# A two-layer transformer block on one core: silu(c) and the squares of the first norm in PSUM, the opening's steps in a written order, the low parts taken one and two feature tiles later

## The chip, the cores and the metric

The kernel runs on one core of one Trainium2 chip. The metric is the device time of one execution in microseconds. Before the change the median of three runs is 1338.73 us (1336.64 to 1339.17).

## What is computed

Two layers act on x of 512 tokens by 1024 features. Each layer has a modulation by a vector c (six parts of 1024 columns), four kinds of attention side by side, an output projection and an MLP. What matters here is the start of layer 0:

```python
c_act = jax.nn.silu(c)
mod = c_act @ w_ada[l] + b_ada[l]
sh1, sc1, g1, sh2, sc2, g2 = [t[:, None, :] for t in jnp.split(mod, N_ADA, axis=-1)]
h = rmsnorm(x, norm_mix_g[l]) * (1.0 + sc1) + sh1
z = h @ w_in[l]
za, zb, zc, zd = split_last(z, [SWA_COLS, MLA_COLS, NSA_COLS, MOBA_COLS])
```

rmsnorm divides by the root of the mean square over the features of a token. Everything is fp32. Products on TensorE are made from two parts of each operand, a high part rounded to fp32r and a low part that holds the rest, and three products stand for one: high by high, low of h by high of w, high of h by low of w.

## The kernel before, in words

The activations lie with features on partitions: x is eight tiles of 128 features by 512 tokens. The change is in the opening of layer 0, the function start (L1085 to L1155), which is called with n = 5: it makes h of all eight feature tiles and the first five groups of 128 columns of z, each in a PSUM bank of its own.

- **silu(c) spread out.** Eight small matmuls put silu(c) on every partition (cb, 128x1024); they land in two PSUM banks named cbp (L173), and DVE copies these to SBUF (L177).
- **x and weights.** The DMA queue of SP brings vecs, ident, x in four transfers, two raw weight tiles of w_in, then in turn raw weights and 16 tiles of w_ada: for each feature tile k a part 1 (the scale) and a part 0 (the shift). The raw weights have four buffers, the w_ada pairs (ada0) four. SP issues in program order, and an issue that waits for a buffer holds those behind it.
- **The norm.** ACT squares the tiles of x (L246), the first into sqacc, the others into SBUF tiles sq; DVE adds them to sqacc (L247). PE sums over partitions (nsum, L1098), DVE scales (rsv, L253), POOL takes the power -1/2 (rs, L257), PE spreads the result (rsb in PSUM, L263).
- **One feature tile.** ada_cols (L188) multiplies a w_ada tile by cb and sums along the row on DVE: one column of mod. Two such steps per feature tile; gs = (mod + 1) * norm weight (L1115); ht = x * gs * rsb (L1121); ACT adds the shift and rounds: hhi (L1124). For the first five tiles ACT writes ht + shift (L1126) and POOL makes hlo (L1127), for the last three DVE makes hlo (L1129).
- **One weight tile.** Weights._split: ACT rounds it (whi, L89), POOL takes the difference (wlo, L91, 128x1024). Eight weight tiles are split in the opening, five of them for it and three for later groups.
- **The products.** 120 matmuls of 128x128 by 512 columns: 5 groups, 8 feature tiles, 3 products. For tiles 0 to 4 they go tile by tile (high by high L1146, low of h L1148; the products with wlo, L1151, wait until tile 2 and then come for tiles 0 to 2 together); the last three tiles go group by group through mm3 (L330 to L332).

The order on an engine is that of a scheduler of the framework; issue_after(x) puts what follows behind x where both are on the same engine, and adds no wait between engines. Behind the opening, ACT and DVE take the five banks apart and PE goes on with the next weight groups (pn, L502).

Of the kernel before, what the change touches and what calls it, by code (L numbers as in the profile page):

```python
# [109 lines left out]
def layer_stack(ctx: ExitStack, tc: tile.TileContext, a, out):  # L110
# [7 lines left out]
    psA = ctx.enter_context(tc.tile_pool(name="psA", bufs=3, space=PSUM))  # L118
    psS = ctx.enter_context(tc.tile_pool(name="psS", bufs=2, space=PSUM))
    psT = ctx.enter_context(tc.tile_pool(name="psT", bufs=2, space=PSUM))  # L120
    psO = ctx.enter_context(tc.tile_pool(name="psO", bufs=1, space=PSUM))

    def mmbank(name):
        return psA.tile([P, 512], F32, tag="mm", name=name)
# [43 lines left out]
    cb = cons.tile([P, D], F32, name="cb")  # L168
    for half in range(2):
        ps = psA.tile([P, 512], F32, tag="mm", name="cbp")  # L170
        for j in range(4):
            k = 4 * half + j
            nc.tensor.matmul(  # L173
                ps[:, j * P : (j + 1) * P], cact[:, k : k + 1].to_broadcast([P, P]), ident,
                start=True, stop=True,
            )
        nc.vector.tensor_copy(cb[:, 512 * half : 512 * half + 512], ps)  # L177

# [5 lines left out]

    def ada_cols(w, l, part, m):

        off = l * VL + OFF_BADA + 8 * part + m
        nc.vector.tensor_tensor_reduce(  # L188
            out=w, in0=w, in1=cb, scale=1.0, scalar=vecs[:, off : off + 1],
            op0=ALU.mult, op1=ALU.add, accum_out=mod[l][:, part, m : m + 1],  # L190
        )

    def ada_start(pool, m):

        raw = pool.tile([P, 2, 1024], F32, tag="ada0", name="ada0", bufs=4)
        for part in (1, 0):
            nc.sync.dma_start(raw[:, part, :], a["wadaP"][m, :, part, :])
            ada_cols(raw[:, part, :], 0, part, m)

# [69 lines left out]
    def sbank(name):  # L269
        return psS.tile([P, 512], F32, tag="sc", name=name)  # L270
# [814 lines left out]
    def start(pool, n):  # L1085

        X["x"] = pool.tile([P, KT, S], F32, name="x0")
        sums = Sums()
        for k in range(0, KT, 2):
            nc.sync.dma_start(X["x"][:, k : k + 2, :], a["xT"][:, k : k + 2, :])  # L1090
        for _ in range(PRELOAD):
            W._load()
        for k in range(KT):
            sums.add(k)
        rsb = psO.tile([P, 512], F32, tag="po", name="rsb0")
        ps = sbank("nsum")
        for j in range(NQ):
            nc.tensor.matmul(  # L1098
                ps[:, j : j + 1], sums.acc[:, j * P : (j + 1) * P], ones, start=True, stop=True
            )  # L1100
# [4 lines left out]
        pss += [psT.tile([P, 512], F32, tag="pt", name="pj") for _ in range(min(n, 5) - 3)]  # L1105
        pss += [sbank("pj") for _ in range(n - 5)]
        W.other_pool.update({i: (pool, 4) for i in range(4)})
        ws = []
        gs = smp.tile([P, KT], F32, tag="gs", name="gs")
        for k in range(KT):  # L1110
            ada_start(pool, k)
            if k < n:
                W.split_ahead, W.load_ahead = AHEAD[k], LAHEAD[k]
                ws.append(W.get())
            nc.vector.scalar_tensor_tensor(  # L1115
# [17 lines left out]
        while W.n_split < n + NSPLIT:  # L1133
            W._split()
        load_consts()
        for _ in range(NADA):
            i = ada_state["i"]
# [5 lines left out]
            ada_state["i"] += 2  # L1143
        for k in range(KG):
            for g in range(n):
                nc.tensor.matmul(pss[g], ws[g][0][:, k, :], hs[k][0], start=k == 0, stop=False)  # L1146
            for g in range(n):
                nc.tensor.matmul(pss[g], ws[g][0][:, k, :], hs[k][1], start=False, stop=False)  # L1148
            for j in [k] if k >= KD else range(KD) if k == KD - 1 else []:
                for g in range(n):  # L1150
                    nc.tensor.matmul(pss[g], ws[g][1][:, j, :], hs[j][0], start=False, stop=False)  # L1151
# [166 lines left out]
```

## Time and profile before

| | |
|---|---|
| median of three runs | 1338.73 us (1336.64 to 1339.17) |
| the profiled execution | 1340.61 us |
| its span | 1338.8 us |
| PE busy | 1257.1 us, 94% |
| DVE busy | 765.2 us, 57% |
| ACT busy | 590.9 us, 44% |
| POOL busy | 512.1 us, 38% |

The span is the stretch from the first to the last instruction in the records of the profiled execution; 1.8 us of its time lie around it. PE is TensorE, DVE VectorE, ACT ScalarE, POOL GpSimd, and SP runs the DMA queue. The shares are means over the whole; the change touches the first 65 us or so. In the windows, the number behind a busy time is that of the instructions, PEclk is the granted clock of TensorE as a share of full speed.

### The profile page before, as it was taken

What the parts mean: (1) busy time and instruction counts of PE and PEld (TensorE: products, weight loads), DVE (VectorE), ACT (ScalarE), POOL (GpSimd) and SP (SyncE); (2) the same over time, 40 slices, a digit from 0 to 9 for tenths busy, and PEclk for the clock granted to TensorE, in tenths of its full rate; (3) what the DMA queues carried; (4) which work ended last, traced back from release to release, by engine and by line L of the source; (5) the groups of instructions that cost most, each with busy time, mean ns of one, the idle gap of its engine ahead of it and who ended that gap; (6) DMA issues with size and microseconds to landing.
All of it is one profiled execution on the core that took longest, in us unless ns stands there. A gap on an engine that the chain in (4) does not pass through costs nothing. (4 is left out here: it accounts for less than half of the span.)

```text
span 1338.8 us, 17560 instructions
## 1 busy us (share of the span) xinstructions
PE 1257.1 (94%) x6500; PEld 1049.3 (78%) x6500; DVE 765.2 (57%) x1609; ACT 590.9 (44%) x1145; POOL 512.1 (38%) x276
## 2 busy tenths in 40 slices
PE   3888999888999999999989899999999999999997
PEld 3676788768988888888889677878888888888886
DVE  6888878978445555454364887677753312213124
ACT  4346768683443132231234657687443313223220
POOL 4432232224344544545433432230534444444441
PEclk9989999999999999999989999999989999999999
DMA  8623233435246766766322221120423333333311
GB/s 334 209 98 127 64 111 111 140 126 206 69 131 185 244 212 209 239 190 204 130 93 90 94 95 64 51 74 11 166 80 94 94 95 95 96 97 98 102 49 64
DMA packets 49766, 168.69 MB, mean 126 GB/s; under 512 B 5648, under 2 KB 8336, under 8 KB 49680
## 3 DMA queue, kind: packets, MB, share of 16 engines
q1 hardware_dynamic: 49680, 167.57, 38.3%
q8 instruction: 51, 0.84, 0.2%
q14 instruction: 35, 0.29, 0.1%
HBM read 163.35 MB, written 4.19 MB: 125 GB/s over the span
## 5 line engine op out<-in xcount | busy, mean ns | idle before, releaser
L91 POOL TENSOR_TENSOR wlo<-raw,whi 128x1024 fp32r<-128x1024 f32 (+3 forms) x186 | 454.9, 2450 | 583.0 <-ACT whi L89 550.9
L89 ACT ACTIVATE whi<-raw 128x1024 fp32r<-128x1024 f32 (+3 forms) x186 | 193.7, 1045 | 437.7 <-PE px L331 237.5
L331 PE MATMUL pj<-hlo,whi 128*128 128x512 f32 (+1 forms) x783 | 297.3, 380 | 8.5 <-DVE hlo L295 8.4
L330 PE MATMUL pj<-hhi,whi 128*128 128x512 f32 (+1 forms) x783 | 296.0, 380 | 2.6 <-ACT hhi L1124 1.2
L332 PE MATMUL pj<-hhi,wlo 128*128 128x512 f32 (+1 forms) x783 | 294.7, 376 | 0.0
L330 PE MATMUL px<-a,whi 128*128 128x512 f32 (+1 forms) x560 | 208.4, 372 | 0.0
L332 PE MATMUL px<-a,wlo 128*128 128x512 f32 (+1 forms) x560 | 208.1, 372 | 0.0
L331 PE MATMUL px<-a,whi 128*128 128x512 f32 (+1 forms) x560 | 207.4, 370 | 0.0
L331 PEld LDWEIGHTS pj<-hlo,whi 128*128 128x128 f32 x783 | 150.8, 193 | 35.5 <-DVE hlo L295 11.4
L330 PEld LDWEIGHTS pj<-hhi,whi 128*128 128x128 f32 x783 | 150.4, 193 | 28.0 <-ACT hhi L1124 2.2
L332 PEld LDWEIGHTS pj<-hhi,wlo 128*128 128x128 f32 x783 | 150.7, 192 | 25.8
L368 DVE SCALAR_TENSOR_TENSOR x<-px,mod,x 128x512 f32<-128x512 f32 (+1 forms) x92 | 62.1, 678 | 171.1 <-PE px L332 162.1
L1071 DVE SCALAR_TENSOR_TENSOR t<-pj,r 128x512 f32<-128x512 f32 x64 | 44.3, 692 | 157.8 <-ACT r L1070 157.8
L188 DVE CUSTOM_DVE_ANT_0 adaw<-adaw,cb,vecs 128x1024 f32<-128x1024 f32 x78 | 105.2, 1349 | 43.8 <-DMA adaw<-in_wadaD 43.7
L332 PEld LDWEIGHTS px<-a,wlo 128*128 128x128 f32 x560 | 105.1, 188 | 19.2
L331 PEld LDWEIGHTS px<-a,whi 128*128 128x128 f32 x560 | 105.1, 188 | 18.8
L330 PEld LDWEIGHTS px<-a,whi 128*128 128x128 f32 x560 | 105.2, 188 | 17.9
L399 DVE TENSOR_TENSOR a<-t,a 128x512 fp32r<-128x512 f32 x64 | 71.8, 1122 | 44.7 <-ACT a L398 44.7
L540 ACT ACTIVATE e<-e,nm 128x256 f32<-128x256 f32 (+3 forms) x160 | 85.9, 539 | 14.6 <-DVE nm L535 14.4
L518 POOL TENSOR_SCALAR e<-e,rc 128x128 f32<-128x128 f32 x40 | 24.3, 608 | 143.2 <-DVE rc L545 67.1
L399 DVE TENSOR_TENSOR pl<-pt,ph 128x512 fp32r<-128x512 f32 (+1 forms) x112 | 65.3, 597 | 4.4 <-ACT ph L398 3.3
L574 PE MATMUL pt<-ident,e 128*128 128x128 f32 x376 | 61.7, 278 | 3.6 <-DVE pl L399 1.5
(236 smaller groups left out, 1932.7 us busy)
## 6 DMA issues: line engine op xcount, KB each, us to landing
adaw<-in_wadaD SPq DMA_DIRECT2D x78, 512.0 KB, 4.4
raw<-in_wup SPq DMA_DIRECT2D x64, 512.0 KB, 3.5
raw<-in_wdown SPq DMA_DIRECT2D x64, 512.0 KB, 3.5
raw<-in_winT SPq DMA_DIRECT2D x28, 512.0 KB, 3.6
ada<-in_wadaP SPq DMA_DIRECT2D x16, 512.0 KB, 7.2
raw<-in_wout SPq DMA_DIRECT2D x16, 512.0 KB, 3.5
x<-in_xT SPq DMA_DIRECT2D x8, 512.0 KB, 5.1
cw<-in_cw SPq DMA_DIRECT2D x8, 512.0 KB, 4.9
```

The source lines that it names most:

```text
L89: self.nc.scalar.activation(vh[0:rows], raw[0:rows], AF.Copy)
L91: eng.tensor_tensor(vl[0:rows], raw[0:rows], vh[0:rows].bitcast(F32), op=ALU.subtract)
L188: nc.vector.tensor_tensor_reduce(out=w, in0=w, in1=cb, scale=1.0, scalar=vecs[:, off : off + 1], op0=ALU.mult, op1=ALU.add, accum_out=mod[ ...
L330: nc.tensor.matmul(ps, wh[:, k, :], hh[:, c], start=first, stop=False)
L331: nc.tensor.matmul(ps, wh[:, k, :], hl[:, c], start=False, stop=False)
L332: nc.tensor.matmul(ps, wl[:, k, :], hh[:, c], start=False, stop=last)
L368: last["dve"] = nc.vector.scalar_tensor_tensor(X["x"][:, m, c], ps, mod[l][:, part, m : m + 1], X["x"][:, m, c], op0=ALU.mult, op1=ALU.add)
L399: last["dve"] = nc.vector.tensor_tensor(lo, src, hi.bitcast(F32), op=ALU.subtract)
L518: nc.gpsimd.tensor_scalar_mul(e, e, r)
L540: nc.scalar.activation(e, e, AF.Exp, bias=nm[:, n : n + 1], scale=-1.0, accum_out=den[:, n : n + 1])
L574: nc.tensor.transpose(pt[:, c : c + P], p[n][:, col : col + P], ident)
L1071: nc.vector.scalar_tensor_tensor(t, ps, 0.0, r, op0=ALU.max, op1=ALU.mult)
```

## The change: what it does

- cb stays in PSUM for the opening (cbP, two banks of a pool of its own, psC); ada_cols takes it as in0 and the w_ada tile in SBUF as in1. One ACT copy of 128x1024 (cb, behind the weight splits) fills the SBUF cb for the later w_ada tiles; then psC is closed and the pool psS takes its banks.
- The squares of tiles 1 to 7 go to PSUM (the three banks of psA), and DVE adds them from there; nsum takes a bank of psT.
- The weight splits of the opening are issued behind POOL's power, and ht of a tile behind both of its ada steps.
- PE takes the low part of h one feature tile after the high part, and the product with wlo two tiles after; the last tile's products and what is left go group by group, six in each.

```diff
-    psS = ctx.enter_context(tc.tile_pool(name="psS", bufs=2, space=PSUM))
...
     cb = cons.tile([P, D], F32, name="cb")
-    for half in range(2):
-        ps = psA.tile([P, 512], F32, tag="mm", name="cbp")
-        for j in range(4):
...
-        nc.vector.tensor_copy(cb[:, 512 * half : 512 * half + 512], ps)
...
-    def ada_cols(w, l, part, m):
+    def ada_cols(w, l, part, m, cv=cb):
...
-        nc.vector.tensor_tensor_reduce(
-            out=w, in0=w, in1=cb, scale=1.0, scalar=vecs[:, off : off + 1],
+        last["ada"] = nc.vector.tensor_tensor_reduce(
+            out=w, in0=cv, in1=w, scale=1.0, scalar=vecs[:, off : off + 1],
...
-        nc.gpsimd.tensor_tensor(r[:, 0:n], v[:, 0:n], mhalf[:, 0:n], op=ALU.pow)
+        last["pow"] = nc.gpsimd.tensor_tensor(r[:, 0:n], v[:, 0:n], mhalf[:, 0:n], op=ALU.pow)
...
+        psC = cps.enter_context(tc.tile_pool(name="psC", bufs=1, space=PSUM))
+        cbP = psC.tile([P, D], F32, name="cbP")
         for k in range(KT):
-            sums.add(k)
+            nc.tensor.matmul(
+                cbP[:, k * P : (k + 1) * P], cact[:, k : k + 1].to_broadcast([P, P]), ident,
+                start=True, stop=True,
+            )
+        acc = wkp.tile([P, S], F32, tag="sqacc", name="sqacc", bufs=1)
+        nc.scalar.activation(acc, X["x"][:, 0, :], AF.Square)
+        for k in range(1, KT):
+            sq = mmbank("sq")
+            nc.scalar.activation(sq, X["x"][:, k, :], AF.Square)
+            nc.vector.tensor_tensor(acc, acc, sq, op=ALU.add)
...
-            ada_start(pool, k)
+            ada_start(pool, k, cbP)
             if k < n:
                 W.split_ahead, W.load_ahead = AHEAD[k], LAHEAD[k]
-                ws.append(W.get())
+                with tc.issue_after(last["pow"].ins):
+                    ws.append(W.get())
...
-            last["dve"] = nc.vector.scalar_tensor_tensor(
-                t, X["x"][:, k, :], gs[:, k : k + 1], rsb, op0=ALU.mult, op1=ALU.mult
-            )
+            with tc.issue_after(last["ada"].ins):
+                last["dve"] = nc.vector.scalar_tensor_tensor(
+                    t, X["x"][:, k, :], gs[:, k : k + 1], rsb, op0=ALU.mult, op1=ALU.mult
+                )
...
+        nc.scalar.activation(cb, cbP, AF.Copy)
+        cps.close()
+        psS = ctx.enter_context(tc.tile_pool(name="psS", bufs=2, space=PSUM))
...
+        for k in range(KT - 1):
+            for w, j, h in ((0, k, 0), (0, k - 1, 1), (1, k - 2, 0)):
+                if j >= 0:
+                    for g in range(n):
+                        part(g, w, j, h)
+        k = KT - 1
         for g in range(n):
-            for k in range(KG, KT):
-                mm3(pss[g], ws[g], hs[k], k, False, k == KT - 1)
+            for w, j, h in (
+                (0, k - 1, 1), (1, k - 2, 0), (1, k - 1, 0), (0, k, 0), (0, k, 1), (1, k, 0)
+            ):
+                part(g, w, j, h)
```

**How it moves instructions.** Line numbers below are each kernel's own; an ISA row is ada_cols' step, a second short one the read of its sum.

POOL at the start of the opening; the first block is before, the second the change. wlo0 to wlo2 are the low parts of the first weight tiles, rs is the power, hlo the low part of feature tile 0.

```order
L91 TENSOR_TENSOR wlo0_208<-raw0_138,whi0_207 128x1024
L257 TENSOR_TENSOR rs_172<-rsv_170,mhalf_96 128x4
L91 TENSOR_TENSOR wlo1_212<-raw1_140,whi1_211 128x1024
L91 TENSOR_TENSOR wlo2_231<-raw2_205,whi2_230 128x1024
L1127 TENSOR_TENSOR hlo_179<-ht_216,hhi_178 128x512
```

```order
L246 TENSOR_TENSOR rs_169<-rsv_167,mhalf_93 128x4
L89 TENSOR_TENSOR wlo0_205<-raw0_122,whi0_204 128x1024
L89 TENSOR_TENSOR wlo1_209<-raw1_124,whi1_208 128x1024
L89 TENSOR_TENSOR wlo2_228<-raw2_202,whi2_227 128x1024
L1130 TENSOR_TENSOR hlo_176<-ht_213,hhi_175 128x512
```

The power now stands ahead of wlo0, the rest is as it was.

PE at the start of the products, before and then the change. hhi_178 and hlo_179 are the parts of feature tile 0 before, hhi_180 the high part of tile 1; in the change these are hhi_175, hlo_176 and hhi_177. whi0 to whi4 are the weight groups, pj their banks.

```order
L1146 MATMUL pj_194<-hhi_178,whi0_207 128x512
L1146 MATMUL pj_195<-hhi_178,whi1_211 128x512
L1146 MATMUL pj_196<-hhi_178,whi2_230 128x512
L1148 MATMUL pj_194<-hlo_179,whi0_207 128x512
L1148 MATMUL pj_195<-hlo_179,whi1_211 128x512
L1148 MATMUL pj_196<-hlo_179,whi2_230 128x512
L1146 MATMUL pj_197<-hhi_178,whi3_234 128x512
L1148 MATMUL pj_197<-hlo_179,whi3_234 128x512
L1146 MATMUL pj_194<-hhi_180,whi0_207 128x512
```

```order
L1151 MATMUL pj_191<-hhi_175,whi0_204 128x512
L1151 MATMUL pj_192<-hhi_175,whi1_208 128x512
L1151 MATMUL pj_193<-hhi_175,whi2_227 128x512
L1151 MATMUL pj_194<-hhi_175,whi3_231 128x512
L1151 MATMUL pj_191<-hhi_177,whi0_204 128x512
L1151 MATMUL pj_192<-hhi_177,whi1_208 128x512
L1151 MATMUL pj_193<-hhi_177,whi2_227 128x512
L1151 MATMUL pj_194<-hhi_177,whi3_231 128x512
L1151 MATMUL pj_191<-hlo_176,whi0_204 128x512
```

Before, the fourth product took the low part of tile 0; now eight products of high parts, of tiles 0 and 1, stand ahead of the first low part.

DVE behind the opening, before and then the change, between two casts and adds of the next stage (ckvg and ckl belong to the key part of one attention, mkh and mkl to its query part, VA to the values).

```order
L717 TENSOR_TENSOR ckvg_475<-ckvg_475,rkb_561 128x512
L487 TENSOR_TENSOR VA_493<-pn_571,VA_493 128x4x64
L399 TENSOR_TENSOR ckl_567<-ckvg_475,ckh_566 128x512
L668 TENSOR_TENSOR cB_681<-pj_198,vecs_85 64x8x31 x4
L487 TENSOR_TENSOR VA_493<-pn_599,VA_493 128x4x64
L668 TENSOR_TENSOR cB_683<-pj_198,vecs_85 64x8x31 x4
L754 CAST mkh_722<-cqh1_472 32x512
L755 CAST mkl_723<-cql1_473 32x512
L487 TENSOR_TENSOR VA_493<-pn_627,VA_493 128x4x64
```

```order
L706 TENSOR_TENSOR ckvg_477<-ckvg_477,rkb_563 128x512
L743 CAST mkh_724<-cqh1_474 32x512
L744 CAST mkl_725<-cql1_475 32x512
L388 TENSOR_TENSOR ckl_569<-ckvg_477,ckh_568 128x512
L476 TENSOR_TENSOR VA_495<-pn_573,VA_495 128x4x64
L657 TENSOR_TENSOR cB_683<-pj_195,vecs_82 64x8x31 x4
L657 TENSOR_TENSOR cB_685<-pj_195,vecs_82 64x8x31 x3
L476 TENSOR_TENSOR VA_495<-pn_601,VA_495 128x4x64
```

The two casts mkh and mkl now stand ahead of ckl and of the adds cB, where they stood behind them.

## Rows read from the trace of the kernel before

**Rows 1.** Windows: us; busy us (instructions) PE, PEld, DVE, ACT, POOL; PEclk, DMA share, GB/s.

```profile
0.00:25.67 25.67, 7.70 (x33) 7.06 (x33) 14.46 (x22) 10.01 (x15) 9.34 (x12) 1.00 0.93 353
25.67:39.90 14.23, 9.76 (x25) 6.09 (x25) 14.06 (x19) 5.38 (x7) 10.78 (x5) 0.88 0.58 186
39.90:64.80 24.90, 23.08 (x98) 17.89 (x98) 20.41 (x30) 10.58 (x17) 10.48 (x6) 1.00 0.73 257
```

**Rows 2.** Timeline of PE: the first products, and the last of the opening.

```profile
25.67 1.65 PE L1146 MATMUL pj<-hhi,whi 128*128 128x512 f32 x3 [4.38 <-ACT hhi L1124]
...
64.39 0.39 PE L332 MATMUL pj<-hhi,wlo 128*128 128x512 f32 x1
```

**Rows 3.** Timeline of DVE: start us, us, operation, [idle before].

```profile
9.88 5.03 DVE L247 TENSOR_TENSOR sqacc<-sqacc,sq 128x512 f32<-128x512 f32 x4
...
21.32 0.75 DVE L1121 SCALAR_TENSOR_TENSOR ht<-x,gs,rsb 128x512 f32<-128x512 f32 x1 [2.84 <-PE rsb L263]
21.99 2.86 DVE L188 CUSTOM_DVE_ANT_0 ada<-ada,cb,vecs 128x1024 f32<-128x1024 f32 x1
...
59.53 0.75 DVE L1129 SCALAR_TENSOR_TENSOR hlo<-ht,mod,hhi 128x512 fp32r<-128x512 f32 x1 [0.79 <-ACT hhi L1124]
```

**Rows 4.** Timeline of POOL in the first 25 us.

```profile
12.00 2.36 POOL L91 TENSOR_TENSOR wlo<-raw,whi 128x1024 fp32r<-128x1024 f32 x1 [11.00 <-ACT whi L89]
17.23 1.92 POOL L257 TENSOR_TENSOR rs<-rsv,mhalf 128x4 f32<-128x4 f32 x1 [2.87 <-DVE rsv L253]
19.12 4.65 POOL L91 TENSOR_TENSOR wlo<-raw,whi 128x1024 fp32r<-128x1024 f32 x2
```

**Rows 5.** One line's instructions: ns smallest/median/largest, first and last start us.

```profile
L188 DVE CUSTOM_DVE_ANT_0 ada<-ada,cb,vecs x16: 1274/1280/3409, 17.0 to 54.1; 128x1024 f32<-128x1024 f32 x16
L1115 DVE SCALAR_TENSOR_TENSOR gs<-mod,vecs x8: 155/708/2170, 18.3 to 56.0; 128x1 f32<-128x1 f32 x8
L1121 DVE SCALAR_TENSOR_TENSOR ht<-x,gs,rsb x8: 744/748/748, 21.3 to 58.0; 128x512 f32<-128x512 f32 x8
L535 DVE CUSTOM_DVE_ANT_0 e<-sc,biasN x64: 266/480/691, 149.6 to 868.0; 128x128 f32<-128x128 f32 x16, 128x256 f32<-128x256 f32 x16, 128x384 f32<-128x384 f32 x16, 128x512 f32<-128x512 f32 x16
```

**Rows 6.** DVE to 60 us, grouped by line: busy us, mean ns of one, idle before.

```profile
L188 DVE CUSTOM_DVE_ANT_0 ada<-ada,cb,vecs 128x1024 f32<-128x1024 f32 x16 | 25.1, 1590 | 0.0
L1115 DVE SCALAR_TENSOR_TENSOR gs<-mod,vecs 128x1 f32<-128x1 f32 x8 | 7.2, 902 | 0.1
```

**Rows 7.** Timeline of ACT: squares, a weight split, the first hhi.

```profile
9.59 1.15 ACT L246 ACTIVATE sq<-x 128x512 f32<-128x512 f32 x2 [0.37 <-DMA x<-in_xT]
...
16.37 1.06 ACT L89 ACTIVATE whi<-raw 128x1024 fp32r<-128x1024 f32 x1 [3.17 <-DMA raw<-in_winT]
...
24.89 0.72 ACT L1124 ACTIVATE hhi<-ht,mod 128x512 fp32r<-128x512 f32 x1 [7.46 <-DVE mod L188]
```

**Rows 8.** Windows, columns as in rows 1: 5 us of the opening.

```profile
15.00:20.00 5.00, 2.63 (x11) 2.58 (x12) 1.52 (x4) 1.06 (x1) 2.77 (x2) 1.00 1.02 417
```

**Rows 9.** Waits of the SP queue to 40.3 us: us, times, longest.

```profile
SPq L197 <- DVE mod L188: 19.0, 4, 7.2
```

**Rows 10.** Timeline of PE: five high by high products at two places.

```profile
37.49 2.50 PE L1146 MATMUL pj<-hhi,whi 128*128 128x512 f32 x5
...
45.25 1.32 PE L1146 MATMUL pj<-hhi,whi 128*128 128x512 f32 x5
```

**Rows 11.** Windows, columns as in rows 1: TensorE idle, and at work again.

```profile
31.70:35.65 3.95, 0.00 (x0) 0.00 (x1) 3.88 (x5) 0.00 (x0) 3.90 (x2) 1.00 0.35 135
36.49:39.90 3.41, 3.38 (x8) 1.75 (x6) 3.38 (x9) 1.44 (x2) 1.63 (x1) 0.50 0.57 154
```

**Rows 12.** Timelines of DVE and PE behind the opening.

```profile
82.65 2.58 DVE L755 CAST mkl<-cql 32x512 fp32r<-32x512 f32 x1
85.95 0.38 PE L734 MATMUL mv<-whi,ckh 128*128 128x256 f32 x1 [2.60 <-ACT gates L691]
...
88.30 0.58 PE L734 MATMUL mv<-whi,ckh 128*128 128x256 f32 x1 [1.74 <-DVE VM L487]
```

More of the change, by code (lines that the diff above doesn't have):

```diff
@@ L25 @@
 PRELOAD = 2
-KG = 5
 NSPLIT = 3
@@ L29 @@
 NJ0 = 1
-KD = 3
 NSTART = 5
@@ L118, in layer_stack @@
     psA = ctx.enter_context(tc.tile_pool(name="psA", bufs=3, space=PSUM))
-    psS = ctx.enter_context(tc.tile_pool(name="psS", bufs=2, space=PSUM))
     psT = ctx.enter_context(tc.tile_pool(name="psT", bufs=2, space=PSUM))
     psO = ctx.enter_context(tc.tile_pool(name="psO", bufs=1, space=PSUM))
+    psS = None
     def mmbank(name):
@@ L168, in layer_stack, with ada_start @@
     cb = cons.tile([P, D], F32, name="cb")
-    for half in range(2):
-        ps = psA.tile([P, 512], F32, tag="mm", name="cbp")
-        for j in range(4):
[L172 to L175, printed above, removed]
-            )
-        nc.vector.tensor_copy(cb[:, 512 * half : 512 * half + 512], ps)
     mod = [cons.tile([P, 6, KT], F32, name=f"mod{l}") for l in range(DEPTH)]
     W = Weights(nc, rawp, hlp, 3, 3)
-    def ada_cols(w, l, part, m):
+    def ada_cols(w, l, part, m, cv=cb):
         off = l * VL + OFF_BADA + 8 * part + m
-        nc.vector.tensor_tensor_reduce(
-            out=w, in0=w, in1=cb, scale=1.0, scalar=vecs[:, off : off + 1],
+        last["ada"] = nc.vector.tensor_tensor_reduce(
+            out=w, in0=cv, in1=w, scale=1.0, scalar=vecs[:, off : off + 1],
             op0=ALU.mult, op1=ALU.add, accum_out=mod[l][:, part, m : m + 1],
         )
-    def ada_start(pool, m):
+    def ada_start(pool, m, cv):
         raw = pool.tile([P, 2, 1024], F32, tag="ada0", name="ada0", bufs=4)
@@ L197, in ada_start @@
             nc.sync.dma_start(raw[:, part, :], a["wadaP"][m, :, part, :])
-            ada_cols(raw[:, part, :], 0, part, m)
+            ada_cols(raw[:, part, :], 0, part, m, cv)
     ada_todo = [(0, part, m) for part in (2, 4, 3, 5) for m in range(KT)]
@@ L1085, in start @@
     def start(pool, n):
+        nonlocal psS
         X["x"] = pool.tile([P, KT, S], F32, name="x0")
-        sums = Sums()
         for k in range(0, KT, 2):
@@ L1092, in start @@
             W._load()
+        cps = ctx.enter_context(ExitStack())
+        psC = cps.enter_context(tc.tile_pool(name="psC", bufs=1, space=PSUM))
+        cbP = psC.tile([P, D], F32, name="cbP")
         for k in range(KT):
-            sums.add(k)
+            nc.tensor.matmul(
[8 more added lines that the diff above has]
+            nc.vector.tensor_tensor(acc, acc, sq, op=ALU.add)
         rsb = psO.tile([P, 512], F32, tag="po", name="rsb0")
-        ps = sbank("nsum")
+        ps = psT.tile([P, 512], F32, tag="pt", name="nsum")
         for j in range(NQ):
             nc.tensor.matmul(
-                ps[:, j : j + 1], sums.acc[:, j * P : (j + 1) * P], ones, start=True, stop=True
+                ps[:, j : j + 1], acc[:, j * P : (j + 1) * P], ones, start=True, stop=True
             )
@@ L1105, in start @@
         pss += [psT.tile([P, 512], F32, tag="pt", name="pj") for _ in range(min(n, 5) - 3)]
-        pss += [sbank("pj") for _ in range(n - 5)]
         W.other_pool.update({i: (pool, 4) for i in range(4)})
@@ L1120, in start @@
             hi, lo = hs[k]
-            last["dve"] = nc.vector.scalar_tensor_tensor(
-                t, X["x"][:, k, :], gs[:, k : k + 1], rsb, op0=ALU.mult, op1=ALU.mult
-            )
+            with tc.issue_after(last["ada"].ins):
+                last["dve"] = nc.vector.scalar_tensor_tensor(
+                    t, X["x"][:, k, :], gs[:, k : k + 1], rsb, op0=ALU.mult, op1=ALU.mult
+                )
             nc.scalar.activation(hi, t, AF.Identity, bias=mod[0][:, 0, k : k + 1])
@@ L1143, in start, with part @@
             ada_state["i"] += 2
[L1144 to L1151, printed above, removed]
+        def part(g, w, k, h):
+            nc.tensor.matmul(
+                pss[g], ws[g][w][:, k, :], hs[k][h], start=(k + w + h == 0),
+                stop=(k == KT - 1 and w == 1),
+            )
+        for k in range(KT - 1):
[4 more added lines that the diff above has]
+        k = KT - 1
         for g in range(n):
-            for k in range(KG, KT):
-                mm3(pss[g], ws[g], hs[k], k, False, k == KT - 1)
+            for w, j, h in (
+                (0, k - 1, 1), (1, k - 2, 0), (1, k - 1, 0), (0, k, 0), (0, k, 1), (1, k, 0)
+            ):
+                part(g, w, j, h)
         return hs, pss
```

## The prediction

> **What bounds the kernel now.** I read the page first: TensorE is busy 94% of the span, so only a stretch in which it stands can give much. The slices show such a stretch at the start, so I read the windows of the opening, then PE's timeline, then DVE's, POOL's and ACT's. To 25.67 us PE does 7.70 us of work, from there to 39.90 it does 9.76 of 14.23, and DVE is busy 14.06 of the same 14.23 [rows 1]: DVE sets the pace. The first product starts at 25.67, after a wait of 4.38 for ACT's hhi; the last starts at 64.39 and takes 0.39, so the opening ends at 64.78 [rows 2], and PE goes straight on. What ends the opening sooner is gained at once, so far as later stages follow.
>
> Why is DVE so busy? Its adds of the squares: four take 5.03 us [rows 3], and in these POOL runs wlo0 from 12.00 to 14.36 [rows 4]. The 16 steps with cb have a median of 1280 ns and a largest of 3409; the eight gs, on one column each, run from 155 to 2170 [rows 5]. But the eight ht, which read rsb from PSUM, all take 744 to 748, and the reductions of L535, which read scores from PSUM, stay below 691 in 64 cases, all four sizes [rows 5]. One case: the step with cb that starts at 21.99 ends at 24.85, 1.1 after POOL's two splits, which run from 19.12 to 23.77 [rows 3, 4], as if most of its own 1.28 had to wait for them. My reading: a DVE instruction with all its tensors in SBUF waits for POOL's split to finish; one with an input in PSUM does not.
>
> **The change part by part.** The sum is made against the profiled execution, 1340.61 us, which is 1.9 above the median of the runs.
>
> 1. The squares in PSUM, and wlo0 behind the power. The last two squares run from 9.59 to 10.74 on ACT [rows 7]. One add unstretched is about 0.69 (an estimate from ht's 0.75, a two-tensor step of the same size [rows 5]), and it follows its square: the adds end near 11.5 instead of 14.91 (9.88 + 5.03 [rows 3]): -3.4. Were a PSUM input no help, wlo0 is still out of the way, as POOL's order shows, so this holds either way. The chain behind (nsum, rsv, power, rsb) took 21.32 - 14.91 = 6.41 and stays: ht of tile 0 starts at 17.9. The two cb copies drop out ahead of all this, beside the wait for x: nothing.
>
> 2. The first hhi. ht ended at 22.07, but hhi started at 24.89 [rows 7], for the shift's step stood behind ht and was stretched to 2.86 [rows 3]. In the change both steps of tile 0 come before ht, in the 2.84 that DVE waits for rsb. So hhi starts at about 18.7 and the first product at about 19.5 instead of 25.67 [rows 2].
>
> 3. DVE from ht of tile 0 to the last hlo: 21.32 to 60.28 (59.53 + 0.75 [rows 3]), 39.0 us. From this: the 16 steps fall from a mean of 1590 to the median, 16 x 0.31 = -5.0 [rows 5, 6]; one of them moves into the wait for rsb, -1.3; the gs still read SBUF alone, 8 x (0.902 - 0.155) = 6.0 of stretch [rows 5, 6]. Bounds: all of it stays, or all goes; since POOL does the same splits in less time I take half, -3.0. Added: the last hlo, from SBUF, now lies beside splits of the later weights, +1.5 (between 0 and the 2.36 of one split [rows 4]); the copy of cb stands on ACT ahead of the last hhi, priced by a weight split of the same 128x1024, 1.06 [rows 7], of which I take +0.7, as ACT is mostly idle. And SP: the fifth raw weight takes raw0's buffer, which wlo0 frees. wlo0 now ends behind the power, near 18.2 instead of 14.36, and everything behind that issue on SP, the w_ada pairs from tile 2 on among it, is held. The queue stays full meanwhile (DMA share 1.02 at 15 to 20 us [rows 8]), so this is bounded by 0 and 3.6 and taken as +1.0. The later pairs come sooner: SP waited 19.0 us for buffers that DVE frees [rows 9]. Sum: 39.0 - 5.0 - 1.3 - 3.0 + 1.5 + 0.7 + 1.0 = 32.9, so the last hlo ends at 50.8.
>
> 4. PE's tail. Behind the last hlo 26 products remain (two of the first group, six of four more), at a pitch of 0.232 ((1.32 - 0.39) / 4 [rows 2, 10]): 6.0, and 0.15 for the last one's length. Before, the tail was 64.78 - 60.28 = 4.5. The opening ends at 57.0 instead of 64.8: **-7.7**. The new order alone adds no product: 120 before and now. It moves low parts and wlo behind, so that PE no longer stands for POOL in front of high parts that are ready; as DVE is the pace, I count nothing beyond the dates above.
>
> 5. Behind the opening. The cast mkl of 32x512 took 2.58, over three times ht's 0.75 for 128x512 [rows 5, 12], which I read as the same stretch; PE waits 2.60 and 1.74 in the next microseconds [rows 12]. In the change both casts stand ahead of ckl. I take -1.0, between -4.3 (both waits go) and +2.0 (the two w_ada steps that follow the opening on DVE, about 1.3 each, fall in a worse place). The later w_ada steps read cb from SBUF as before: 0.
>
> Total -8.7: 1331.9 for a profiled execution, **1330.0** for the median.
>
> [...] In the rows, a reduction from PSUM at 512 columns takes at most 0.69 [rows 5], half of the 1.28 for 1024 columns from SBUF, so I put no surcharge into the sum. [...]
>
> **The rivals.**
>
> A. The change does not do what it says: a step that reads cb from PSUM and w from SBUF is stretched all the same, since one of its two inputs still comes from SBUF. For it: the 3409 ns step shows how much there is to lose, and no row before shows this very mix at 1024 columns. Against it: ht has the same mix (x from SBUF, rsb from PSUM) and stays at 744 to 748. Then DVE keeps its 39.0 us, with the same splits in it; the 3.4 of the adds and the 1.3 are eaten by later data (3.6) and the longer tail (1.5): about 1339, within 0.2%, up to 2.3 more where the stretch grows. Chance 0.07.
>
> B. The other side: TensorE at its low clock. It is fed sooner, but in small bursts with DVE's steps between. [...] Chance 0.05. [...]
>
> C. The gain is given back: PE comes to the attention stage 7.7 us sooner, and the waits at 82 to 92 us grow, as gates and the values' sums come from ACT and DVE, which have all the rest of their work to do. For it: PE waits there already [rows 12]. Against it: that work starts from the banks of the opening, so it moves forward too. With 5.5 to 7.5 given back: 1336 to 1338. Chance 0.12.
>
> **How the numbers follow.** My forecast has 0.76. Its unknowns all at their good ends (gs without stretch, both waits gone) give 1323.7; all at their bad ends (gs as before, data 3.6 late, +2.0 behind) 1338.6. They will not fall together, so I take 1324.5 to 1337.0; this takes in half of C and leaves out A, B and the other half, 0.18. About 0.2%, 2.7 us, is what a measurement can tell from no change: faster, under 1336.0, has the forecast and a quarter of C, 0.79; within 0.2% the rest of C and most of A, 0.14; slower B and the bad part of A, 0.07.
>
> **What would show it.** In the changed profile: adds at 0.7 each with the last ending near 11.5; 16 steps with cbP all near 1.28; ht of tile 0 at 17.9; a first product at 19.5; the last of the opening at about 57; PEclk 1.00 from 40 us on. I am wrong if the steps with cbP are stretched beside POOL (A), if PEclk shows 0.5 through the opening (B), if the opening ends near 57 and the waits for gates or VM have grown by as much (C), or if the w_ada tiles come so late that DVE waits for DMA.

## The result, and the profile of the changed kernel

The changed kernel takes a median of 1329.82 us (1328.21 to 1331.56, four runs); the kernel before took 1337.68 beside it (four runs). The ratio is 0.9943, with a 95% interval of 0.9924 to 0.9962: faster by 0.6%. The profiled execution of the change took 1331.56 us, 9.05 less than that of before; its span is 1329.8.

The windows of the opening, changed kernel, columns as in [rows 1]:

```profile
10.00:31.00 21.00, 12.05 (x34) 9.14 (x35) 18.23 (x27) 10.34 (x13) 16.26 (x9) 0.51 1.00 377
31.00:56.96 25.96, 24.52 (x106) 19.37 (x105) 20.67 (x33) 11.60 (x18) 8.82 (x6) 1.00 0.79 290
```

PE's timeline: the first products, the last wait of the opening, its last product (against [rows 2]):

```profile
20.67 2.50 PE L1151 MATMUL pj<-hhi,whi 128*128 128x512 f32 x4 [2.88 <-ACT hhi L1127]
...
46.24 1.43 PE L1151 MATMUL pj<-hhi,whi 128*128 128x512 f32 x5 [1.44 <-ACT hhi L1127]
...
56.57 0.39 PE L1151 MATMUL pj<-hhi,wlo 128*128 128x512 f32 x1
```

In these two executions the opening ends at 56.96 instead of 64.78, 7.8 sooner; the other 1.2 of the 9.05 come behind it. DVE's timeline (against [rows 3]):

```profile
7.67 4.64 DVE L1096 TENSOR_TENSOR sqacc<-sqacc,sq 128x512 f32<-128x512 f32 x6 [0.28 <-ACT sq L1095]
...
15.73 2.27 DVE L1117 SCALAR_TENSOR_TENSOR gs<-mod,vecs 128x1 f32<-128x1 f32 x1
17.92 1.27 DVE L177 CUSTOM_DVE_ANT_0 ada<-cbP,ada,vecs 128x1024 f32<-128x1024 f32 x1
...
19.12 0.74 DVE L1124 SCALAR_TENSOR_TENSOR ht<-x,gs,rsb 128x512 f32<-128x512 f32 x1
...
49.05 0.75 DVE L1132 SCALAR_TENSOR_TENSOR hlo<-ht,mod,hhi 128x512 fp32r<-128x512 f32 x1 [1.02 <-ACT hhi L1127]
```

One line's instructions, ns smallest/median/largest (against [rows 5]):

```profile
L177 DVE CUSTOM_DVE_ANT_0 ada<-cbP,ada,vecs x16: 1266/1274/1284, 14.4 to 45.4; 128x1024 f32<-128x1024 f32 x16
L1117 DVE SCALAR_TENSOR_TENSOR gs<-mod,vecs x8: 143/607/2265, 15.7 to 46.6; 128x1 f32<-128x1 f32 x8
```

The groups of gs and of two later steps, whose cb lies in SBUF: busy us and mean ns (against [rows 6]):

```profile
L177 DVE CUSTOM_DVE_ANT_0 ada<-cb,ada,vecs 128x1024 f32<-128x1024 f32 x2 | 2.5, 1280 | 0.0
L1117 DVE SCALAR_TENSOR_TENSOR gs<-mod,vecs 128x1 f32<-128x1 f32 x8 | 7.3, 918 | 0.1
```

All 16 steps with cbP take 1.27 to 1.28, while POOL is at work beside them as before; the eight gs are held as much as before, 7.3 us in all (before 7.2). POOL's timeline (against [rows 4]):

```profile
14.65 1.02 POOL L246 TENSOR_TENSOR rs<-rsv,mhalf 128x4 f32<-128x4 f32 x1 [13.65 <-DVE rsv L242]
15.63 6.99 POOL L89 TENSOR_TENSOR wlo<-raw,whi 128x1024 fp32r<-128x1024 f32 x3
```

The gs of tile 0 starts at 15.73, 0.1 behind wlo0's start at 15.63, and ends at 18.00, where wlo0 ends too (6.99 us for three splits, about 2.33 each): it is held for the whole of wlo0, and with it the second step and ht. PE's waits behind the opening, to 120 us (against [rows 12]), us in all, times, longest:

```profile
PE mv L723 <- DVE VM L476: 1.4, 1, 1.4
PE rkb L252 <- POOL rs L246: 1.1, 1, 1.1
PE mv L723 <- ACT gates L680: 0.6, 1, 0.6
```

The SP queue's waits to 40.3 us (against [rows 9]):

```profile
SPq L186 <- DVE mod L177: 7.4, 4, 2.7
SPq L72 <- POOL wlo L89: 6.8, 1, 6.8
```

Before, the second of these was:

```profile
SPq L74 <- POOL wlo L91: 3.5, 1, 3.5
```

The first cast mkl behind the opening (against [rows 12]):

```profile
68.19 0.41 DVE L744 CAST mkl<-cql 32x512 fp32r<-32x512 f32 x1
```

The two waits for gates and VM fell from 4.3 to 2.0, a wait of 1.1 for rkb is new: 1.2 less. SP waits 7.4 instead of 19.0 for w_ada buffers, and 6.8 instead of 3.5 for wlo0 to free the buffer of the fifth raw weight.

Behind the opening the kernels differ by more than this 1.2. From its end to the end of the span the profiled executions take 1274.0 us before, 1272.8 in the change, and from 1265.2 to 1276.4 in the runs below.

### The profile page after: what moved, and what is told of

Read it like the earlier page. It is cut to its first block, busy times and chain, and to the rows that moved or that the text cites. A ratio compares the mean times of both kernels' runs of the same rounds, so it can differ in the third digit from the quotient of the medians.

```text
span 1329.8 us, 17565 instructions
## 1 busy us (share of the span) xinstructions
PE 1256.4 (94%) x6500; PEld 1050.3 (79%) x6500; DVE 749.2 (56%) x1607; ACT 591.4 (44%) x1146; POOL 508.1 (38%) x276
## 5 line engine op out<-in xcount | busy, mean ns | idle before, releaser
L320 PE MATMUL pj<-hlo,whi 128*128 128x512 f32 (+1 forms) x768 | 290.6, 378 | 8.5 <-DVE hlo L284 8.4
L319 PE MATMUL pj<-hhi,whi 128*128 128x512 f32 (+1 forms) x768 | 290.6, 379 | 1.2 <-ACT hhi L283 1.0
L321 PE MATMUL pj<-hhi,wlo 128*128 128x512 f32 (+1 forms) x768 | 289.0, 376 | 0.0
L320 PEld LDWEIGHTS pj<-hlo,whi 128*128 128x128 f32 x768 | 147.8, 192 | 34.8 <-DVE hlo L284 11.3
L321 PEld LDWEIGHTS pj<-hhi,wlo 128*128 128x128 f32 x768 | 147.8, 192 | 25.5
L319 PEld LDWEIGHTS pj<-hhi,whi 128*128 128x128 f32 x768 | 147.4, 192 | 24.8 <-ACT hhi L283 1.4
L177 DVE CUSTOM_DVE_ANT_0 adaw<-cb,adaw,vecs 128x1024 f32<-128x1024 f32 x78 | 103.0, 1320 | 46.9 <-DMA adaw<-in_wadaD 46.9
```

Source lines behind the costliest of these rows:

```text
L177: last["ada"] = nc.vector.tensor_tensor_reduce(out=w, in0=cv, in1=w, scale=1.0, scalar=vecs[:, off : off + 1], op0=ALU.mult, op1=ALU.add, ...
L319: nc.tensor.matmul(ps, wh[:, k, :], hh[:, c], start=first, stop=False)
L320: nc.tensor.matmul(ps, wh[:, k, :], hl[:, c], start=False, stop=False)
L321: nc.tensor.matmul(ps, wl[:, k, :], hh[:, c], start=False, stop=last)
```

## The experiments

Two theories stood against each other. The first: DVE is held by POOL only where all its tensors lie in SBUF, so the place of cb makes the gain. The second: the written orders (POOL's power first, ht behind both steps, low parts later on PE) make it. Each run is given by its median, its ratio to before on the same chip with the interval, and the end of its opening in the profile (before 64.78, the change 56.96).

**cb back in SBUF.** The change, but the opening's steps read an SBUF copy that DVE makes.

```diff
+        for half in range(2):
+            c = slice(512 * half, 512 * half + 512)
+            nc.vector.tensor_copy(cb[:, c], cbP[:, c])
...
-            ada_start(pool, k, cbP)
+            ada_start(pool, k, cb)
...
-        nc.scalar.activation(cb, cbP, AF.Copy)
```

> The change with one thing undone: DVE copies cb from PSUM to SBUF at the start, and the 16 steps of the opening read it there. Theory (a DVE instruction with all tensors in SBUF is held until POOL's split ends, one with an input in PSUM is not): the 16 steps go from a median and largest of 1.27 and 1.28 us to a mean of about 1.5 with some over 2.5, the last hlo from 49.8 to about 54, the opening from 57.0 to about 60 to 61; the median 3 to 4 us above the change's. Rival 1 (the new orders on PE, DVE and POOL make the gain, PSUM is only a place): the opening ends within 0.7 us of 57.0, which is the cost of the copies at most. Rival 2 (DMA sets the pace of the w_ada steps now): stretched steps are hidden by the wait for w_ada tiles, the last hlo moves by less than 1 us.

Measured: 1339.07 us, ratio 1.0003 (0.9986 to 1.0019): nothing is left of the gain. The opening ends at 67.54. DVE's timeline, the copies and the last adds:

```profile
9.16 1.28 DVE L1093 COPY cb<-cbP 128x512 f32<-128x512 f32 x2
10.36 3.06 DVE L1099 TENSOR_TENSOR sqacc<-sqacc,sq 128x512 f32<-128x512 f32 x4
```

DVE to 62 us, grouped by line (busy us, mean ns):

```profile
L177 DVE CUSTOM_DVE_ANT_0 ada<-cb,ada,vecs 128x1024 f32<-128x1024 f32 x16 | 25.9, 1633 | 0.0
L1120 DVE SCALAR_TENSOR_TENSOR gs<-mod,vecs 128x1 f32<-128x1 f32 x8 | 10.4, 1296 | 0.1
```

POOL's timeline:

```profile
15.75 1.92 POOL L246 TENSOR_TENSOR rs<-rsv,mhalf 128x4 f32<-128x4 f32 x1 [14.75 <-DVE rsv L242]
17.63 8.37 POOL L89 TENSOR_TENSOR wlo<-raw,whi 128x1024 fp32r<-128x1024 f32 x3
```

The same 16 steps, in the same order, take a mean of 1633 ns instead of 1274, and POOL's power and first three splits take 1.92 and 8.37 instead of 1.02 and 6.99: the two engines hold each other. The operands stand in the order of the change here too (cb first, the w_ada tile second), so that order is not what helps. Both rivals fall. The effect was larger than the theory had it, since gs and POOL grow too, and the copies make the adds end at 13.42 instead of 12.31. With cb in SBUF, the written orders alone end the opening 2.8 later than before.

**Squares back in SBUF.** The change, but the squares go to SBUF tiles.

```diff
-            sq = mmbank("sq")
+            sq = tmp_tile("sq")
```

> The change with one thing undone: the squares of tiles 1 to 7 in SBUF tiles again. Theory: POOL's power stands ahead of wlo0, so nothing runs on POOL beside the adds, and they take 0.69 each from SBUF too; the four SBUF tiles in place of three PSUM banks let ACT run ahead, so the adds end at 12.0 to 12.4 as now, the opening at 57.0 within 0.4. Rival (PSUM makes the adds fast): the adds are stretched as before, end near 14 to 15, and the opening ends 1.5 to 2.5 us later.

Measured: 1330.72 us, ratio 0.9945 (0.9927 to 0.9964), as the change. DVE's adds and the steps of tile 2:

```profile
6.95 5.48 DVE L1096 TENSOR_TENSOR sqacc<-sqacc,sq 128x512 f32<-128x512 f32 x7 [3.23 <-ACT sq L1095]
...
25.23 1.28 DVE L177 CUSTOM_DVE_ANT_0 ada<-cbP,ada,vecs 128x1024 f32<-128x1024 f32 x1 [0.61 <-DMA ada<-in_wadaP]
26.56 2.23 DVE L1117 SCALAR_TENSOR_TENSOR gs<-mod,vecs 128x1 f32<-128x1 f32 x1
```

The adds end at 12.43, 0.1 later than in the change: their place is worth nothing here. The opening ends at 59.34, outside what was expected, for another reason: the w_ada tile lands 0.34 later, gs of tile 2 starts at 26.56 instead of 26.22, and now meets a split of POOL (2.23 instead of 0.16). In a second execution the change itself does this too (below).

**PE's old order.** The change, but with the products in the order of before.

```diff
-        for k in range(KT - 1):
-            for w, j, h in ((0, k, 0), (0, k - 1, 1), (1, k - 2, 0)):
...
+        for k in range(5):
+            for g in range(n):
+                nc.tensor.matmul(pss[g], ws[g][0][:, k, :], hs[k][0], start=k == 0, stop=False)
+            for g in range(n):
+                nc.tensor.matmul(pss[g], ws[g][0][:, k, :], hs[k][1], start=False, stop=False)
...
+                mm3(pss[g], ws[g], hs[k], k, False, k == KT - 1)
```

> The change with PE's old order of products (low part of h with its own tile, wlo of tiles 0 to 2 after tile 2, then all of the last three tiles group by group). Theory (DVE's dates set the end, 120 products either way): DVE, ACT and POOL keep their dates within 0.5 us; PE stands for POOL's hlo again for some microseconds, but catches up before the last tiles, and the opening ends at 57.0 to 58.5. Rival (the order on PE is what gives the gain): the opening ends at 61 or later.

Measured: 1329.48 us, ratio 0.994 (0.9919 to 0.9961), as the change. PE waits 2.8 for hlo again and still ends the opening at 56.25, although DVE's last hlo comes 2.3 later (52.08). So PE's order does not make the gain; with its 26 products behind the last hlo its tail is longer, 7.2 us in the change against 4.2 here.

**wlo0 ahead of the power.** The change, but POOL's power is issued behind wlo0.

```diff
+            self.lo_op = eng.tensor_tensor(
...
+        W._split()
+        with tc.issue_after(W.lo_op.ins):
+            r = rstd_cols(ps, NQ, [(0, NQ, 1.0 / D)])
```

> The change with POOL's order turned back at one place: wlo0 ahead of the power. Theory: the adds read PSUM and are not held, so they stay at 0.69 and end near 12.3; wlo0 runs from about 12.2 to 14.6 and the power starts at 14.6 as now, so it costs nothing there; the fifth raw weight's transfer is issued near 14.7 instead of 18.0, the dip of the DMA at 16 to 19 us goes, and DVE no longer waits 0.39 for a w_ada tile at 24.5. The opening ends at 56 to 57.0. Rival (the power's place ahead of wlo0 is worth its 3.4 us): the adds or the power come later and the opening ends 2 to 3 us later.

Measured: 1325.92 us, ratio 0.992 (0.9895 to 0.9945); the opening ends at 55.88. POOL's timeline:

```profile
12.17 2.35 POOL L89 TENSOR_TENSOR wlo<-raw,whi 128x1024 fp32r<-128x1024 f32 x1 [11.18 <-ACT whi L87]
14.79 1.01 POOL L246 TENSOR_TENSOR rs<-rsv,mhalf 128x4 f32<-128x4 f32 x1 [0.27 <-DVE rsv L242]
```

DVE's timeline, gs of tile 0, and gs of tile 1, which took 1.53 in the change:

```profile
15.88 2.26 DVE L1119 SCALAR_TENSOR_TENSOR gs<-mod,vecs 128x1 f32<-128x1 f32 x1
...
21.24 0.16 DVE L1119 SCALAR_TENSOR_TENSOR gs<-mod,vecs 128x1 f32<-128x1 f32 x1
```

wlo0 fits in ahead of the power, which starts 0.14 later than in the change. No DVE step waits for a w_ada tile any more, and SP's wait for wlo0 is 3.5 again. The gs of tile 0 is held as before, now by the next split. So the power's place brings no gain. That it is a loss is not clear of the noise here: the intervals of this run and of the change overlap (0.9924 to 0.9962 there), and of the 7.1 us between the two profiled spans (1322.7 and 1329.8) only 1.1 lie in the opening. Beside gs on ACT (below) it is clearer.

**gs on ACT.** The change, but ACT makes gs.

```diff
-            nc.vector.scalar_tensor_tensor(
-                gs[:, k : k + 1], mod[0][:, 1, k : k + 1], 1.0, vecs[:, OFF_NMIX + k : OFF_NMIX + k + 1],
-                op0=ALU.add, op1=ALU.mult,
-            )
+            nw = vecs[:, OFF_NMIX + k : OFF_NMIX + k + 1]
+            nc.scalar.activation(gs[:, k : k + 1], mod[0][:, 1, k : k + 1], AF.Identity, scale=nw, bias=nw)
```

> The change with gs = (mod + 1) * norm weight made by ACT (scale and bias both the norm weight) and no longer by DVE, where the eight gs took 7.3 us in the change, up to 2.27 for one column. Theory (gs is held because all its tensors are in SBUF; DVE and then PE set the end): ht of tile 0 starts near 17.9 instead of 19.12, no DVE instruction of the opening but the last hlo is stretched, the last hlo ends at 46 to 48 instead of 49.8, and the opening ends at 54.5 to 56. Rival 1 (DMA has become the pace, its share is 1.01 from 20 to 40 us): DVE waits for w_ada tiles as much as gs gave, the last hlo moves by less than 1 us. Rival 2 (ACT's gs comes late, behind weight splits): ht waits for ACT, the opening ends later than 57.0.

Measured: 1326.33 us, ratio 0.991 (0.9877 to 0.9942); the opening ends at 55.92. DVE to 62 us, the group of the steps (busy us, mean ns, idle before):

```profile
L177 DVE CUSTOM_DVE_ANT_0 ada<-cbP,ada,vecs 128x1024 f32<-128x1024 f32 x16 | 20.1, 1277 | 3.8 <-DMA ada<-in_wadaP 3.8
```

DVE's timeline, the last hlo:

```profile
46.66 2.01 DVE L1130 SCALAR_TENSOR_TENSOR hlo<-ht,mod,hhi 128x512 fp32r<-128x512 f32 x1 [1.10 <-ACT hhi L1125]
```

Both the theory and its first rival hold in part: the last hlo ends at 48.67, 1.1 sooner, and of the 7.3 us that gs had taken 3.8 turn up as waits for w_ada tiles.

**PE's new order alone, on the kernel before.** The same lines the other way round.

```diff
-        for k in range(KG):
...
+        for k in range(KT - 1):
+            for w, j, h in ((0, k, 0), (0, k - 1, 1), (1, k - 2, 0)):
```

> The kernel before with the change's order of products on PE alone. Theory (DVE's dates set the end): the last hlo stays near 60.3; PE no longer stands 4.0 us for POOL's hlo, but behind the last hlo 26 products remain instead of 19, so the opening ends at 64.8 to 67, and the median is 0 to 2 us above before. Rival (the order on PE is what gives the gain): the opening ends at 62 or sooner, the median 3 us or more below before.

Measured: 1336.85 us, ratio 0.9982 (0.9964 to 1.0000). The opening ends at 66.96, 2.2 later than before, as the longer tail says; the wait for gates behind it falls from 2.6 to 0.6. The rival's 3 us and more do not come.

**Only cb in PSUM.** The change, with squares in SBUF, wlo0 ahead of the power, ht ahead of the second step, and PE's old order; to the lines for wlo0 and PE above come these:

```diff
-            sq = mmbank("sq")
+            sq = tmp_tile("sq")
...
-                with tc.issue_after(last["pow"].ins):
-                    ws.append(W.get())
+                ws.append(W.get())
...
-            with tc.issue_after(last["ada"].ins):
-                last["dve"] = nc.vector.scalar_tensor_tensor(
+            last["dve"] = nc.vector.scalar_tensor_tensor(
```

> Of the change only cb in PSUM for the opening (with its copy on ACT and the later pool): squares in SBUF, wlo0 ahead of the power, ht ahead of the second w_ada step, PE's old order. Theory (the source of cb makes most of the gain): the 16 steps all take 1.27 to 1.29; the adds are held by wlo0 as before and end near 14.5 to 15, the first hhi starts near 22 to 23; the last hlo ends at 51 to 54, the opening at 55.5 to 58.5, the median 5 to 8 us below before. Rival (the orders make the gain): the opening ends later than 61.

Measured: 1324.67 us, ratio 0.9893 (0.9863 to 0.9922). The opening ends at 55.56. DVE's timeline, the adds:

```profile
7.18 5.48 DVE L1096 TENSOR_TENSOR sqacc<-sqacc,sq 128x512 f32<-128x512 f32 x7 [3.54 <-ACT sq L1095]
```

POOL's timeline, the first split:

```profile
12.26 2.61 POOL L89 TENSOR_TENSOR wlo<-raw,whi 128x1024 fp32r<-128x1024 f32 x1 [11.27 <-ACT whi L87]
```

This one part gains more than the whole change (the pair at the end shows it on one chip). It also shows what made the adds late before: here they read SBUF, and wlo0 stands where it stood, and yet they end at 12.66 and meet only its first 0.4 us. What is gone are DVE's two cb copies, 1.4 us among the adds, which had pushed the last add into wlo0. With the copies, but wlo0 out of the way (the first run), the adds ended at 13.42; with both, at 14.91.

**gs on ACT and wlo0 first, together.** The lines of both runs above, on the change:

```diff
+            nc.scalar.activation(gs[:, k : k + 1], mod[0][:, 1, k : k + 1], AF.Identity, scale=nw, bias=nw)
...
+        W._split()
+        with tc.issue_after(W.lo_op.ins):
+            r = rstd_cols(ps, NQ, [(0, NQ, 1.0 / D)])
```

> The change with gs on ACT and wlo0 ahead of the power, both at once. Theory: the two gains add up as far as DVE is the pace: w_ada tiles come sooner by the earlier transfer of the fifth raw weight, ht of tile 0 near 17.9, the last hlo at 44 to 47, then PE with its low clock at the start becomes the bound: the opening ends at 53 to 55. Rival (DMA at a share of 1.0 is the pace): within 0.5 us of the better of the two alone.

Measured: 1321.60 us, ratio 0.9870 (0.9842 to 0.9898), the lowest median of all: 0.7% below the change by the ratios of both to before, and 4.7 us below gs on ACT alone on the same chip. The opening ends at 52.13, the last hlo at 45.75 (43.75 + 2.00). In the opening the two together bring 4.8 us, more than the 1.1 and 1.0 of each alone, and PE has only 1.9 us of waits for hhi left. From 31 us on it is never idle there: PE has become the bound.

**The same with PE's old order.** To that come the loops of before:

```diff
-            for w, j, h in ((0, k, 0), (0, k - 1, 1), (1, k - 2, 0)):
...
+            for g in range(n):
+                nc.tensor.matmul(pss[g], ws[g][0][:, k, :], hs[k][1], start=False, stop=False)
```

> cb in PSUM, gs on ACT, wlo0 ahead of the power, and PE's old order of products. Theory (with the new order the end waits for 26 products behind the last hlo, with the old one for 19, but PE stands for POOL's hlo early; and PE has become the bound once gs is off DVE): the opening ends at 51 to 54, within 1.5 us of the same kernel with the new order (52.1). Rival 1 (the old order's shorter tail decides): at or below 50.5. Rival 2 (the new order is needed once DVE is fast): above 54.5.

Measured: 1326.77 us, ratio 0.9919 (0.9896 to 0.9942). The opening ends at 52.64, as the theory says. The time is worse by what comes behind it, 1276.4 us of span against 1268.0 with the new order. PE's waits there:

```profile
PE mv L723 <- ACT gates L680: 2.6, 1, 2.6
PE mv L723 <- DVE VM L476: 1.7, 1, 1.7
```

These are as long as before; with the new order they are 0.6 and 1.4. That makes 2.3 of the 8.4 us; the rest was not traced. The two were timed on different chips, but the next run, on this one's chip, is faster by 4.3 us with the new order too. So here the new order gains behind the opening, which it did not in the change.

**The same with PE kept busy.** Five products whose result is not used, placed where PE stands ahead of the first products, added to the fastest kernel.

```diff
+        warm = psT.tile([P, 512], F32, tag="pt", name="warm")
+        with tc.issue_after(wop.ins):
+            for j in range(3):
+                wop = nc.tensor.matmul(warm, ident, X["x"][:, 7, :], start=True, stop=True)
...
+        with tc.issue_after(last["bc"].ins):
+            wop = nc.tensor.matmul(warm, ident, X["x"][:, 7, :], start=True, stop=True)
```

> cb in PSUM, gs on ACT, wlo0 ahead of the power, the new order on PE, and five added products of ident with a tile of x, into a bank that is overwritten later: three between the spread of silu(c) and nsum, one ahead of rsb, one behind it. They compute nothing that is used. Theory (PE has become the bound there and pays for its granted clock of 0.55 to 0.60 from 10 to 30 us): PEclk is 1.00 from 20 us on, the products of the first tiles have a pitch of 0.23 instead of 0.43, and the opening ends 1.5 to 3 us sooner than 52.1, unless the added products delay rsb. Rival (DVE's dates set the end, the low clock costs nothing): the opening ends at 52.1 within 0.5.

Measured: 1322.46 us, ratio 0.9894 (0.9873 to 0.9915). The opening ends at 51.82. The first three products take 0.96 instead of 1.65 us, but the granted clock from 20 to 30 us rose only from 0.60 to 0.83, and PE waits 1.5 for a weight split on ACT instead. The theory falls at this size: 0.3 us.

**The change and cb in PSUM alone, again, on one chip.** Both unaltered.

> The change once more, unaltered, beside the kernel with cb in PSUM alone, on one chip. Theory (cb in PSUM makes all of the gain, the rest of the change costs a little in the opening): median 1328 to 1331 us, the opening ends at 56.5 to 59.5 (one gs beside POOL's fifth split makes it 2 us sooner or later), 1.5 us or more above the kernel with cb alone. Rival (the rest of the change helps, the lower time of the kernel with cb alone was that of its chip): at or below the kernel with cb alone.

> Only cb in PSUM, unaltered, beside the change, on one chip. Theory: the opening ends at 55 to 56 again and the median is 1324 to 1327, 1.5 to 5 us below the change. Rival (its earlier time was that of the chip, or of the low-clock stretches behind the opening in those runs): within 1 us of the change, or above it.

Measured: the change 1329.44 us, ratio 0.9941 (0.9921 to 0.9962), opening to 59.37; cb alone 1324.70 us, ratio 0.9897 (0.9877 to 0.9916), opening to 55.74. On one chip the rest of the change costs 4.7 us. Of the 9.2 us between their spans (1332.4 and 1323.2) 3.6 lie in the opening; there the change's w_ada tile comes 0.78 late and gs of tile 2 meets a split (2.06), as in the run with the squares in SBUF. A window of this second profile of the change:

```profile
10.00:31.00 21.00, 11.26 (x31) 8.14 (x31) 17.79 (x24) 9.23 (x12) 15.17 (x8) 1.00 0.97 364
```

PE's timeline, its first products and the last of the opening:

```profile
20.84 2.50 PE L1151 MATMUL pj<-hhi,whi 128*128 128x512 f32 x4 [2.88 <-ACT hhi L1127]
...
58.98 0.39 PE L1151 MATMUL pj<-hhi,wlo 128*128 128x512 f32 x1
```

One program, two executions: with PEclk 0.51 from 10 to 31 us its opening ended at 56.96, with 1.00 at 59.37. This does not show what the clock costs, for PE's pace is the same in both. The first four products take 2.50 us in both, and from the start of the next four (25.31 and 25.48) to the start of the product behind them 1.87 us pass in both, 0.47 each, twice the later pitch of 0.232. The record of the clock differs and the products do not. That the slow pace costs nothing in the change is seen elsewhere: at 46.24 PE waits 1.44 for hhi, so by then it had caught up with DVE.

The other 5.5 us lie behind the opening (1273.0 against 1267.5 us of span; the first pair of profiles has 1272.8 and 1266.9). PE's waits in the 125 us that begin 170 us behind each opening, first the change, then cb alone:

```profile
PE rsb L266 <- DVE sqacc L236: 3.5, 1, 3.5
PE po L579 <- DVE pl L388: 2.9, 4, 2.0
```

```profile
PE rsb L266 <- DVE sqacc L236: 1.8, 1, 1.8
PE po L579 <- DVE pl L388: 0.7, 2, 0.3
```

These two make 3.9 of the 5.5. The same waits with wlo0 ahead of the power, again in the 125 us from 170 us behind the opening:

```profile
PE rsb L266 <- DVE sqacc L236: 1.1, 1, 1.1
PE po L579 <- DVE pl L388: 0.7, 2, 0.3
```

They are as short there, with one part of the change turned back, and also in the run with cb back in SBUF (1.1 and 0.7), so no one part makes them by itself. The order of later DVE and ACT work differs between the kernels; how it makes these waits was not tried.

## Why the prediction was right, and where it was not

The time, the direction and the end of the opening came as forecast: 1330.0 against 1329.82, 57.0 against 56.96, -1.0 against -1.2 behind the opening. The main step, the cure of the 16 steps, is right. The agreement to a tenth is luck: ht of tile 0 came 1.2 later than forecast, the stretch from there to the last hlo was 2.2 shorter and PE's tail 1.0 longer, and these cancel. The forecast was -8.7 from 1338.73; beside the change, before took 1337.68, so the change was -7.9. One sum is a tenth off: 64.8 less 57.0 is 7.8, not 7.7.

Rivals A and B fell: the steps with cbP are not held (1284 ns at most), and the low clock (0.51 from 10 to 31 us) cost nothing, since PE waits 1.44 for hhi again at 46.24. C did not decide this kernel; the waits that it names came back to their old length in one of the experiments, gs on ACT with PE's old order. By its steps:

- **The steps (part 3).** Right: 1274 ns each, and the first run shows that cb's place alone is worth the gain. There POOL's own work is stretched as well (8.37 us for three splits instead of 6.99). What makes the two engines hold each other, no run shows.
- **The adds (part 1).** Mis-sized a little, and with half of its cause missing. They end at 12.31, not 11.5: DVE has six of them in a row from 7.67, so DVE and not the last square sets the date; -2.6 instead of -3.4. I said that wlo0 behind the power frees them and that the two cb copies cost nothing. The runs show that the copies matter as much: with them but without wlo0 the adds end at 13.42 (the first run), with both at 14.91. Without the copies the adds are in time whatever holds the squares and wherever wlo0 stands (12.31 to 12.85).
- **The first hhi (part 2).** 1.2 late: hhi starts at 19.89, the first product at 20.67 instead of 19.5. The power became faster (1.02 for 1.92), but wlo0 right behind it holds gs of tile 0 for 2.27. I had put both steps into the wait for rsb and forgotten gs between them. With wlo0 ahead of the power the next split holds it just as long (2.26).
- **The gs (part 3).** The reason for the term of -3.0 was wrong: the gs take 7.3 us in all, 7.2 before. But the longest of them, of tile 0, now lies ahead of ht of tile 0, where it makes the first hhi late; the seven behind it take 5.1 instead of 7.1. So the stretch that I summed lost 2.0.
- **What made up for it.** The last hlo was not held (0.75, I had +1.5). That was timing: it starts at 49.05 and the next split at 49.13; in the four runs with gs on ACT it took 1.99 to 2.02. The w_ada tiles came 0.39 late instead of +1.0, and with the copy of cb on ACT the last hlo waits 0.2 longer for its hhi (1.02 for 0.79) instead of +0.7. From ht of tile 0 to the last hlo DVE takes 30.7 us (19.12 to 49.80), 2.2 less than my 32.9. In the second profile, where gs of tile 2 met a split, it takes 32.9 (19.30 to 52.21). So the opening of the same program ends at 56.96 or 59.37.
- **The tail (part 4).** 7.2 us from the last hlo to the end, not 6.15: behind its wait for hhi at 46.24 PE has 45 products to do and never stands again, and 45 x 0.232 = 10.4 from there is the end. I had let the 26 products start with the last hlo.
- **Behind the opening (part 5).** The reading of the casts holds: mkl takes 0.41 instead of 2.58, and PE's waits for gates and VM fall by 2.3. In every other profile where the first mkl takes under 1 us the two waits are 0.5 to 0.9 and 1.4 to 1.5; only in the two runs that turn PE's order back, on the change and on the kernel with gs on ACT, does it take 2.0 or more, and there they come to 4.2 and 4.3. That all of it nets to 1.2, so near the -1.0, is luck: kernels that differ only in parts of the change lie up to 11 us apart there.
- **The PSUM operand.** I put no surcharge for it into the sum, and none shows: 1266 to 1284 ns with cb in PSUM, while the two later steps of the changed kernel with cb in SBUF have a mean of 1280.
- **What I did not see.** Taken together, the rest of the change is a loss, 4.7 us on one chip. I gave the power's place the gain of the adds and +1.0 for later data. The adds do not need it; SP waits 6.8 instead of 3.5 to load the fifth raw weight, and gs of tile 1 meets a split (1.53 instead of 0.16). Turned back, the kernel is at 1325.92. The new order on PE, which I priced at nothing, lengthens the tail and gains nothing in the opening; behind it, it is worth some 4 to 5 us, but only in the kernel with gs on ACT. ht behind both steps was not tried by itself.

## What to carry to other kernels

Where GpSimd works beside VectorE, look at the spread of one line's durations: a smallest and a largest far apart, with the ends on POOL's ends, can mark VectorE instructions that are held: in the change gs took 143 to 2265 ns, and the longest ended with wlo0 at 18.00. Here, moving one input of the long ones to PSUM cured them (a largest of 1284 ns instead of 3409); the tiny ones between them stayed held (7.3 us for eight, 7.2 before) until ACT made them. After such a change, test its other parts one by one against it: here one part made more than the whole, and an order that was worth nothing in one kernel was worth some 4 us in another. And price what is queued between two moved steps, however small: a one-column instruction waited 2.27 us.

## What the runs showed that I had not expected

- POOL is held as well: its power on 128x4 takes 1.92 us beside a step from SBUF (before and the first run) and 1.02 beside one from PSUM; its first three splits 8.37 against 6.99.
- A tile that lands 0.34 us later can cost 2 us: gs of tile 2 took 0.16 when it started at 26.22 and 2.23 at 26.56.
- The granted clock on record for the same program in the same stretch was 0.51 in one execution and 1.00 in another, yet the same products followed each other at the same pace (0.47 us apart, twice the later 0.232). So a record of 1.00 does not prove full pace; the starts of the products have to be read beside it.
